# A load's last row on the other DMA queue, and one copy in place of two, in an RMSNorm that writes every row twice

## The chip, the cores and the metric

The kernel runs on one core of one Trainium2 chip. A core has engines with a queue of instructions each: TensorE (PE, not used here), VectorE (DVE), ScalarE (ACT), GpSimd (POOL) and SyncE (SP), and 16 DMA engines that move data between the memory (HBM) and the on-chip memory of 128 partitions. A DMA is issued by an instruction on SP or ACT; DMAs from SP stand in the profile as queue q1, those from ACT as queue q10. The metric is the device time in microseconds of one execution, the median of several.

## The reference

The input `x` has 8 x 512 rows of 2048 float32 values. Each row is normalised by its root mean square and multiplied by `gamma`, and every row appears twice, one after the other, in the output:

```python
x_rep = np.repeat(x, 2, axis=1)
rms = np.sqrt((x_rep ** 2).mean(axis=-1, keepdims=True) + 1e-6)
x_norm = x_rep / rms
return (x_norm * gamma[None, None, :]).astype(np.float32)
```

So 33.6 MB are read and 67.1 MB are written.

## The kernel before

The 4096 rows are cut into four loads of 1024 rows. A load puts eight consecutive rows (k = 0 to 7) into each of the 128 partitions, 8 x 8,192 bytes a partition; per DMA engine these are eight partitions. A store writes four rows with their copies, again eight rows' worth per partition and 8.4 MB, so there are eight stores. All live in one on-chip tile `y` of 24 rows per partition, with three regions that begin at rows 0 (`first`), 8 (`second`) and 16 (`third`).

The function `four` (line 93) handles two loads: load n goes to `first + K` (rows 4 to 11 of `y`), load n + 1 to `third`. It is called twice, for loads 0 and 1 (line 147) and 2 and 3 (line 148). The order of instructions on each engine is the order in which they are written; there is no scheduler. For each group of rows the steps are:

- `squares` (line 59): ACT squares each row and sums it (line 65), then takes the root of the mean of all rows of the group (line 69).
- `scale` (line 72): DVE takes the reciprocal (line 78) and, row by row, multiplies the row by it and by `gamma` (line 79), writing to every second row of the output region.
- `repeat` (line 84): ACT or DVE copies the scaled rows to the rows between (line 86).
- `store` (line 54): SP issues the store.

In the first call of `four` the first load is cut in two DMAs: rows 0 to 6 of each partition, and row 7 (`cuts` is (7, 8)). `load` (line 49) issues the pieces in reverse, so row 7 goes first, both on SP's queue; load 1 follows in one piece. ACT's queue has only gamma. The function `constants` (line 126) fetches gamma in three DMAs on it, into partition 0 of `y`: 16 pieces of 126 values, and the last 32 values in two DMAs of 64 bytes each. POOL then spreads gamma over all partitions, the main part at line 138 and the last 32 values at line 142, into `gamma_b`. Line 79 needs all of `gamma_b`.

Row 7 is first needed by the squares of the second half of load 0 (line 105, rows 7, 6, 5, 4), after the first half (rows 0 to 3, lines 99 to 104) has been scaled and copied. `at_once` is 1 in the first call and 2 in the second: there the copies of line 101 are of one row or of two.

The loads 2 and 3 are issued when the stores that read their regions have finished; the stores are issued in order on SP, as their copies are done.

Of the kernel before, what the change touches and what calls it, by code (L numbers as in the profile page):

```python
# [1 line left out]

# [4 lines left out]


@with_exitstack
def kernel(  # L10
    ctx: ExitStack,
    tc: tile.TileContext,
    x: bass.AP,
    gamma: bass.AP,
    out: bass.AP,
):
    nc = tc.nc
    P = nc.NUM_PARTITIONS
    f32 = mybir.dt.float32
    Act = mybir.ActivationFunctionType  # L20
    Alu = mybir.AluOpType

    B, S, D = x.shape
    Bo, So, Do = out.shape
    R = So // S
    assert R == 2 and D == Do and B == Bo and So == S * R
    eps = 1e-6
    inv_d = 1.0 / float(D)


    K = 4
    N = B * S
    ntiles = N // (P * K)
    assert N % (P * K) == 0 and ntiles == 8
    H = 2
    x_t = x.rearrange("b s d -> (b s) d").rearrange("(n p k) d -> n p k d", p=P, k=H * K)
    out_t = out.rearrange("b s d -> (b s) d").rearrange("(n p h j) d -> n h p (j d)", p=P, h=H, j=K * R)

    singles = ctx.enter_context(tc.tile_pool(name="singles", bufs=1))
    rows = ctx.enter_context(tc.tile_pool(name="rows", bufs=1))  # L40
    junk = ctx.enter_context(tc.tile_pool(name="junk", bufs=1, space=bass.MemoryType.PSUM))
    small = ctx.enter_context(tc.tile_pool(name="small", bufs=4))

    y = rows.tile([P, 3 * K * R, D], f32, name="y")
    first, second, third = 0, K * R, 2 * K * R

    def load(n, at, cuts=(H * K,)):
        ends = (0, *cuts)  # L50
        for k0, k1 in reversed(list(zip(ends, ends[1:]))):
            nc.sync.dma_start(out=y[:, at + k0 : at + k1, :], in_=x_t[n][:, k0:k1, :])  # L52

    def store(n, h, to):
        nc.sync.dma_start(
            out=out_t[n, h], in_=y[:, to : to + K * R, :].rearrange("p j d -> p (j d)")
        )

    def squares(at, rows):

        n = len(rows)
        ss = small.tile([P, n], f32, name=f"ss{n}")
        for c, k in enumerate(rows):
            sq = junk.tile([P, D], f32, name="sq")
            nc.scalar.activation(  # L65
                out=sq[:], in_=y[:, at + k, :], func=Act.Square, accum_out=ss[:, c : c + 1]
            )
        rms = small.tile([P, n], f32, name=f"rms{n}")
        nc.scalar.activation(out=rms[:], in_=ss[:], func=Act.Sqrt, scale=inv_d, bias=eps_t[:])  # L69
        return rms  # L70

    def scale(at, to, rows, rms, at_once=K):
        n = len(rows)
        rstd = small.tile([P, n], f32, name=f"rstd{n}")
        for c, k in enumerate(rows):
            if c % at_once == 0:
                part = slice(c, min(c + at_once, n))
                nc.vector.reciprocal(out=rstd[:, part], in_=rms[:, part])  # L78
            nc.vector.scalar_tensor_tensor(  # L79
                out=y[:, to + R * k, :], in0=y[:, at + k, :], scalar=rstd[:, c : c + 1],  # L80
                in1=gamma_b[:], op0=Alu.mult, op1=Alu.mult,
            )

    def repeat(to, k0, k1, copy):
        y_r = y[:, to + R * k0 : to + R * k1, :].rearrange("p (k r) d -> p k r d", r=R)
        copy(out=y_r[:, :, 1, :], in_=y_r[:, :, 0, :])  # L86

    ctx.enter_context(tc.manual_schedule())

    half = K // 2  # L90
    up, down = list(range(K)), list(range(K - 1, -1, -1))

    def four(n, constants, cuts, at_once):


        load(n, first + K, cuts)
        constants()
        load(n + 1, third)
        for rows, n_at_once in ((up[:half], half), (up[half:], at_once)):
            scale(first + K, first, rows, squares(first + K, rows), n_at_once)  # L100
        for k in range(0, half, at_once):
            repeat(first, k, k + at_once, nc.scalar.copy)
        repeat(first, half, K, nc.vector.tensor_copy)
        store(n, 0, first)
        scale(second, second, down, squares(second, down))
        for k in range(half, K, at_once):
            repeat(second, k, k + at_once, nc.scalar.copy)
        repeat(second, 0, half, nc.vector.tensor_copy)
        store(n, 1, second)
        roots = [squares(third + h * K, up) for h in range(H)]  # L110
        scale(third, first, up, roots[0])
        repeat(first, 0, half, nc.scalar.copy)
        repeat(first, half, K, nc.scalar.copy)
        store(n + 1, 0, first)
        scale(third + K, third, up, roots[1])
        repeat(third, 0, K, nc.scalar.copy)
        store(n + 1, 1, third)

    gamma_b = singles.tile([P, D], f32, name="gamma_b")
    G, E = 16, 2  # L120
    C = D // G - E
    gamma_s = y[0:1, 0:2, :].rearrange("p k (c d) -> p (k c) d", c=G // 2)
    gamma_t = y[0:1, 2, :]
    eps_t = singles.tile([P, 1], f32, name="eps_t")

    def constants():
        nc.gpsimd.memset(eps_t, eps)  # L127
        nc.scalar.dma_start(
            out=gamma_s[0:1, :, :C],
            in_=gamma[: G * C].rearrange("(p c d) -> p c d", p=1, c=G),  # L130
        )
        for c in range(E):
            at = G * C + c * G
            nc.scalar.dma_start(
                out=gamma_t[0:1, c * G : (c + 1) * G],
                in_=gamma[at : at + G].partition_broadcast(1),
            )
        nc.gpsimd.partition_broadcast(  # L138
            out_ap=gamma_b[:, : G * C].rearrange("p (c d) -> p c d", c=G),
            in_ap=gamma_s[0:1, :, :C],  # L140
        )
        nc.gpsimd.partition_broadcast(out_ap=gamma_b[:, G * C :], in_ap=gamma_t[0:1, : E * G])  # L142

        root = singles.tile([P, 1], f32, name="root")[:]
        nc.scalar.activation(out=root, in_=eps_t[:], func=Act.Sqrt)  # L145

    four(0, constants, (H * K - 1, H * K), 1)
    four(2, lambda: None, (H * K,), half)


# [1 line left out]
_INS = ['x', 'gamma']  # L152
_OUTS = [((8, 1024, 2048), 'float32')]


# [23 lines left out]
```

## Time and profile before

| what | value |
|---|---|
| median of 3 runs | 238.25 us (238.18 to 238.48) |
| profiled execution | 239.85 us, span 238.0 us |
| DMA, mean | 423 GB/s |
| DVE busy | 84.4 us, 35% of the span |
| ACT busy | 110.2 us, 46% |
| POOL busy | 2.9 us, 1% |
| load 0, rows 0 to 6: issue to landing | 21.5 us |
| load 0, row 7: issue to landing | 4.9 us |
| gamma, main part: issue to landing | 5.1 us |
| loads 1 to 3: issue to landing, median | 40.5 us |
| stores: issue to landing, median | 24.9 us |

The span is the time from the first to the last event of the profiled execution; 1.85 us of its time lie around the span. A busy time is the sum over an engine's instructions. The time to landing of a DMA holds its wait behind other DMAs. In the timeline each row has the start in us, the time in us, the engine (SPq and ACTq are DMA issues), the line of the kernel, the operation, its operands, how many instructions were merged in the row, and in brackets the idle time before it and what ended that. In the DMA view a queue's row has packets, MB and the time of its packets as a share of 16 engines over the window; a long packet counts where it starts.

### The profile page before, as it was taken

The numbers are of one execution on the slowest core, as the hardware profiler recorded it, in microseconds if no ns is written. First come the engines' busy times: TensorE is split into PE (matmuls) and PEld (weight loads), VectorE is DVE, ScalarE is ACT, GpSimd is POOL, SyncE is SP. The second block draws the span as 40 slices with busy tenths as digits, with TensorE's granted clock in tenths as the row PEclk, the third lists the DMA queues.
The fourth block names the chain that finished last, engine by engine and source line by source line (L and its number), as shares of the span: only waits on it lengthen the run. The fifth ranks groups of instructions, "written<-read, shape, count | busy, mean of one in ns | idle before, by whom it ended". The sixth has DMA issues, their size and how long they took to land.

```text
span 238.0 us, 228 instructions
## 1 busy us (share of the span) xinstructions
DVE 84.4 (35%) x47; ACT 110.2 (46%) x88; POOL 2.9 (1%) x7
## 2 busy tenths in 40 slices
DVE  0000495792799400000000006937918992000000
ACT  2001999299996560000000039891999957400000
POOL 0300000000000000000000000000000000000000
DMA  8997989898998989898999999999998999999994
GB/s 332 463 453 340 529 352 529 352 518 363 463 419 365 518 352 529 352 529 352 419 386 430 441 441 441 430 452 408 463 419 386 474 408 463 419 441 441 441 441 176
DMA packets 1909, 100.68 MB, mean 423 GB/s; under 512 B 244, under 2 KB 244, under 8 KB 244
## 3 DMA queue, kind: packets, MB, share of 16 engines
q1 hardware_dynamic: 1872, 100.66, 98.4%
q10 hardware_dynamic: 36, 0.01, 0.0%
q14 instruction: 1, 0.01, 0.0%
HBM read 33.56 MB, written 67.11 MB: 423 GB/s over the span
## 4 chain that ended last, share of the span: by engine, by line
DMA 46%; ACT 28%; DVE 11%; issue 1%; SPq 0%; DVEq 0%; ACTq 0%
DMA y<-in_x_dram 26%; DMA out_dram<-y 20%; ACT sq L65 17%; DVE y L79 11%; ACT y L86 11%; ACT rms L69 1%; DVE rstd L78 0%; SPq L52 0%; DVEq L79 0%; ACTq L86 0%
## 5 line engine op out<-in xcount | busy, mean ns | idle before, releaser
L65 ACT ACTIVATE sq<-y 128x2048 f32<-128x2048 f32 x32 | 60.1, 1878 | 73.2 <-DMA y<-in_x_dram 72.5
L79 DVE SCALAR_TENSOR_TENSOR y<-y,rstd,gamma_b 128x2048 f32<-128x2048 f32 x32 | 73.8, 2349 | 2.2 <-DMA out_dram<-y 1.6
L86 ACT COPY y<-y 128x4096 f32<-128x4096 f32 (+2 forms) x12 | 42.8, 3599 | 18.9 <-DVE y L79 18.9
L78 DVE RECIPROCAL rstd<-rms 128x4 f32<-128x4 f32 (+2 forms) x11 | 1.9, 169 | 111.2 <-ACT rms L69 111.2
L86 DVE COPY y<-y 128x4096 f32<-128x4096 f32 x4 | 9.2, 2293 | 0.1
L65 ACT ACTIVATION_READ_ACCUMULATOR sq<-y 128x1 f32 x32 | 6.0, 186 | 0.0
L69 ACT ACTIVATE rms<-ss,eps_t 128x4 f32<-128x4 f32 (+1 forms) x10 | 3.0, 297 | 0.3
L145 ACT ACT_TABLE_LOAD x1 | 1.3, 1283 | 2.3 <-issue 2.3
L138 POOL PARTITION_BROADCAST gamma_b<-y x1 | 2.3, 2257 | 5.1 <-DMA y<-in_gamma_dram 5.1
L142 POOL PARTITION_BROADCAST gamma_b<-y x1 | 0.3, 310 | 6.2 <-DMA y<-in_gamma_dram 6.2
L145 ACT ACTIVATE root<-eps_t 128x1 f32<-128x1 f32 x1 | 0.2, 203 | 0.0
L127 POOL MEMSET eps_t<- 128x1 f32 x1 | 0.1, 98 | 0.3 <-POOLq L163 0.3
L163 POOL MEMSET const-bfloat16-1.0<- 128x1 bf16 x1 | 0.1, 101 | 0.0
L163 POOL MEMSET const-uint8-127<- 128x1 uint8 x1 | 0.1, 101 | 0.0
L163 POOL MEMSET const-float32-0.0<- 128x1 f32 x1 | 0.1, 98 | 0.2 <-issue 0.2
L163 POOL MEMSET const-float32-1.0<- 128x1 f32 x1 | 0.1, 98 | 0.0
## 6 DMA issues: line engine op xcount, KB each, us to landing
y<-in_x_dram SPq DMA_DIRECT2D x1, 7168.0 KB, 21.5
y<-in_x_dram SPq DMA_DIRECT2D x1, 1024.0 KB, 4.9
out_dram<-y SPq DMA_DIRECT2D x8, 24.9
y<-in_x_dram SPq DMA_DIRECT2D x3, 40.5
y<-in_gamma_dram ACTq DMA_DIRECT2D x2, 0.1 KB
y<-in_gamma_dram ACTq DMA_DIRECT2D x1, 7.9 KB, 5.1
```

The costliest lines, as they stand in the source:

```text
L65: nc.scalar.activation(out=sq[:], in_=y[:, at + k, :], func=Act.Square, accum_out=ss[:, c : c + 1])
L69: nc.scalar.activation(out=rms[:], in_=ss[:], func=Act.Sqrt, scale=inv_d, bias=eps_t[:])
L78: nc.vector.reciprocal(out=rstd[:, part], in_=rms[:, part])
L79: nc.vector.scalar_tensor_tensor(out=y[:, to + R * k, :], in0=y[:, at + k, :], scalar=rstd[:, c : c + 1], in1=gamma_b[:], op0=Alu.mult, op ...
L86: copy(out=y_r[:, :, 1, :], in_=y_r[:, :, 0, :])
L127: nc.gpsimd.memset(eps_t, eps)
L138: nc.gpsimd.partition_broadcast(out_ap=gamma_b[:, : G * C].rearrange("p (c d) -> p c d", c=G), in_ap=gamma_s[0:1, :, :C],)
L142: nc.gpsimd.partition_broadcast(out_ap=gamma_b[:, G * C :], in_ap=gamma_t[0:1, : E * G])
L145: nc.scalar.activation(out=root, in_=eps_t[:], func=Act.Sqrt)
L163: nc = _bacc.Bacc("TRN2", target_bir_lowering=False, num_devices=1)
```

## The change

The first load still has two pieces, but they are issued in rising order and on two queues: rows 0 to 6 on SP's, row 7 on ACT's. As `load` is called ahead of `constants`, row 7 stands before gamma's three DMAs there. Loads with one piece go on SP's queue as before. The second edit replaces the loop over the first two copies on ACT by a single copy of two rows; it differs only in the first call of `four`, since the second call already copied two rows at once.

```diff
     def load(n, at, cuts=(H * K,)):
         ends = (0, *cuts)
-        for k0, k1 in reversed(list(zip(ends, ends[1:]))):
-            nc.sync.dma_start(out=y[:, at + k0 : at + k1, :], in_=x_t[n][:, k0:k1, :])
+        for k0, k1, queue in zip(ends, cuts, (nc.sync, nc.scalar)):
+            queue.dma_start(out=y[:, at + k0 : at + k1, :], in_=x_t[n][:, k0:k1, :])
...
-        for k in range(0, half, at_once):
-            repeat(first, k, k + at_once, nc.scalar.copy)
+        repeat(first, 0, half, nc.scalar.copy)
         repeat(first, half, K, nc.vector.tensor_copy)
```

## The prediction

> **What bounds the kernel now.** I read the page first: the span, the slices of the DMA engines, the queues.
>
> ```profile
> span 238.0 us, 228 instructions
> DMA  8997989898998989898999999999998999999994
> q1 hardware_dynamic: 1872, 100.66, 98.4%
> q10 hardware_dynamic: 36, 0.01, 0.0%
> ```
>
> The 16 DMA engines are busy in every slice. SyncE's queue, q1, holds 98.4% of their time; DVE and ACT are at 35% and 46%. The kernel is a stream of 100.66 MB that is never let run dry, so an edit costs time only where it lets the stream stop. The chain of waits (46% DMA, 28% ACT) runs back through compute because each store is issued by compute, but no gap shows there. So the second reading is where the stream is nearest to stopping. That is the first store, whose data must pass through compute while load 1 is still landing. The timeline of that stretch:
>
> ```profile
> 0.72 1.34 SPq L52 DMA_DIRECT2D y<-in_x_dram  x3
> 0.72 0.60 ACTq L128 DMA_DIRECT2D y<-in_gamma_dram  x1
> 1.35 0.91 ACTq L134 DMA_DIRECT2D y<-in_gamma_dram  x2
> 5.92 2.26 POOL L138 PARTITION_BROADCAST gamma_b<-y  x1 [5.12 <-DMA y<-in_gamma_dram]
> 14.36 0.31 POOL L142 PARTITION_BROADCAST gamma_b<-y  x1 [6.18 <-DMA y<-in_gamma_dram]
> 22.69 1.88 ACT L65 ACTIVATE sq<-y 128x2048 f32<-128x2048 f32 x1 [18.90 <-DMA y<-in_x_dram]
> 27.35 4.62 DVE L79 SCALAR_TENSOR_TENSOR y<-y,rstd,gamma_b 128x2048 f32<-128x2048 f32 x2
> 31.22 3.68 ACT L86 COPY y<-y 128x2048 f32<-128x2048 f32 x2
> 36.92 2.29 DVE L86 COPY y<-y 128x4096 f32<-128x4096 f32 x1
> 39.29 16.20 SPq L55 DMA_DIRECT2D out_dram<-y  x2
> ```
>
> gamma is spread over the partitions by 14.67 us and is first used at 27.35: 12.7 us of room. The first store is issued at 39.29. A cold queue needed 1.01 us from issue (0.72) to its first packet (1.73, packet records), so the store could start at 40.30. The packet records show load 1 leaving the 16 engines between 40.96 and 41.48. The room before the stream stops is therefore 0.66 to 1.18 us; I take 0.85.
>
> The third reading decides: how the two queues share an engine. DMA view for three windows, 1.5 to 4.6, 4.6 to 5.2 and 5.2 to 14.0 us (columns: packets, MB, share):
>
> ```profile
> q1 hardware_dynamic: 122, 1.00, 92.8%
> ...
> q1 hardware_dynamic: 38, 0.97, 375.7%
> q10 hardware_dynamic: 32, 0.01, 6.0%
> ...
> q1 hardware_dynamic: 64, 3.67, 96.2%
> q10 hardware_dynamic: 4, 0.00, 0.0%
> ```
>
> The packet records give the order inside these windows. On each engine it is: row 7's eight packets of 8,192 bytes (0.306 us each) and its 4-byte semaphore write; gamma's 504 bytes and its semaphore write; then the packets of rows 0 to 6, 57,344 bytes and 2.113 us each. So no gamma packet came between row 7's, although both DMAs were issued at 0.72. On the one engine that carries gamma's two last pieces their four packets (64 B, 4 B, 64 B, 4 B) go one at a time behind one 57,344-byte packet each. That is why line 142 starts only at 14.36. Two rules follow: a DMA whose issue is done first (SP's took 0.37 us, ACT's 0.60) gets its nine packets in first; once both queues are backed up they alternate packet by packet, whatever the sizes.
>
> **The change part by part.** First part: SP loses one of its first three issues (row 7, 0.37 us) and starts with rows 0 to 6 at 0.72. ACT gains row 7's issue, and gamma's three move behind it, in time and in q10. Bytes and packets stay the same. On one engine load 0 and load 1 need 8 x 2.113 + 8 x 0.306 + 8 x 2.414 = 38.7 us however they are mixed, so load 1 still leaves at about 41.2. The landing of rows 0 to 6 moves from 22.67 to between 19.5 (row 7 wholly behind) and 22.6 (mixed). An earlier landing buys nothing if gamma is what comes last. One issue less on SP buys nothing either: the queue is full at once.
>
> What is late next is gamma. q10 now holds, on the engine with the last pieces, 15 packets: row 7's nine, gamma's two, then four. q1 holds nine of rows 0 to 6 and nine of load 1 (eight of 65,536 bytes, 2.414 us, and the semaphore write), and then nothing until the first store, which itself needs gamma. By the first rule, SP's nine packets of rows 0 to 6 pass first, as SP's nine of row 7 did before: both DMAs start at 0.72 again. Then row 7's alternate with load 1's. If no more than six of q10's 15 slip through ahead of that, nine or more remain against load 1's nine, so gamma's last piece gets in when load 1 is through, at about 41.2. From its packet to line 142 took 0.72 us (13.64 to 14.36), line 142 takes 0.31, the hop 0.05: DVE starts at 42.3 in place of 27.35. That is 14.95 us later; the 0.85 of room comes off: 14.1 us in which the DMA engines have nothing.
>
> Bounds of this unknown: gamma could stay early (row 7 wholly ahead, as in the trace of before; cost 0), or even gamma's main piece could be done only when load 1 is through on all engines. Then line 138 starts at 41.48 + 0.72 = 42.2, and 2.26 + 0.31 + 0.05 more make DVE start at 44.8, a cost of 17.45 - 0.85 = 16.6. I take 14.1, which lies between the mixtures below and that end. Nothing lies below zero: DMA work is the same and the stream has no gap that an earlier row could close.
>
> Who waits while gamma is late: DVE's first multiply, behind it all of DVE's queue; on ACT the copy of line 86, and behind it the squares of the second half; POOL has nothing else; SP stands at the first store.
>
> Second part: on ACT two copies (3.68 us together) become one of 4096 elements, 3.60 by the by-form groups (mean 3598 ns): 0.1 us less. But it waits for both multiplies: its start moves from 3.87 us after DVE's start (31.22 - 27.35, ACT was busy until then) to 4.67, and its end from 7.55 to 8.27, so the squares of the second half start 0.7 to 0.8 us later. The first store waits for DVE's copy (11.9 after DVE's start), so it is not touched. The second store is issued 27.8 us after DVE's start now, 28.6 then, and its packets could start at 29.6; the first store keeps the engines until 12.9 + 8 x 2.414 = 32.2. Hidden, with 2.6 us to spare; if that cover were gone it would cost 0.8. The third store (75.52 now, 1.0 to its packets, the second's last packets end at 79.9) has 3.4 us now and keeps 1.7.
>
> The sum goes on the profiled execution's own time: 239.85 (span 238.0 and 1.85 around it) + 14.1 + 0 = 253.95. The median of the runs is 1.60 under the profiled one: 252.35, say 252.4.
>
> **A rule weighed.** The rows say one packet at a time (64 bytes against 57,344). The Trainium skill, "DMA: Bandwidth & Descriptors", section "Queues, rings and completion order", says that each DMA engine goes round its queues and drains a whole packet, typically 9 to 17 descriptors, before it switches. By that rule row 7 would go as one turn, and all of load 1 as one turn ahead of gamma, which is the second rival below, 254.9. In this trace the order of row 7 and gamma fits that rule; the four pieces between single 57,344-byte rows do not.
>
> **The rivals.**
> One by one from the first packet on. For it: the last pieces were let in after a single 57,344-byte packet. Against: row 7's nine went ahead of gamma undivided. If one packet of rows 0 to 6 leads, the 15th packet of q10 follows the 15th of q1, which is the sixth of load 1: 1.73 + 0.5 (the first packets took up to 1.1 us, not 0.31) + 16.9 + 2.4 + 6 x 2.414 = 36.0, DVE at 37.1, cost 9.75 - 0.85 = 8.9: 247.2. With a lead of two: 249.6. With three or more: 252.4. With ACT ahead by one packet: 244.8.
>
> Whole transfers in turn. All of load 1 passes before gamma's main piece, or too few of row 7's nine slip through: 238.25 + 16.6 = 254.9.
>
> No change: row 7 gets its nine packets in before rows 0 to 6 do. For it: both issues start at 0.72, and small packets are soon done (2.5 us). Then gamma has six packets against eight of rows 0 to 6 and is there by 1.73 + 0.5 + 2.4 + 8 x 2.113 = 21.5 at the latest, DVE-ready at 22.6, under 27.35. The time is then 238.2. It decides at a gamma_b ready before 27.35 + 0.85 = 28.2. Against: SP's issue took 0.37 us and ACT's 0.60, side by side. Letting one queue drain several small packets per turn would do the same; the four single pieces speak against it.
>
> **How the numbers follow.** Gamma behind load 1: 0.57, of which 0.32 for 252.4 (the likeliest) and 0.25 for 254.9, 0.10 of that for whole transfers in turn. One by one: 0.27 (0.13 near 249.6, 0.10 near 247.2, 0.04 near 244.8). No change: 0.16. The range leaves out no change and the 0.04: 246.8 to 255.3, which holds 0.8. A change under 0.2% (0.5 us) is about what a measurement of this kernel cannot tell from none. No change is split over both sides of zero: faster 0.04, since nothing in the stream shortens, same 0.12; slower 0.84. The slower cases' own range is 244.5 to 255.3.
>
> **What would show it.** Line 142 of before (141 after) starts near 41.9 and not 14.36; the first multiply waits for POOL and starts near 42.3; the first store is issued near 54.2; the DMA slices show one gap, from about 41 to 55, and are full after it. Landing of rows 0 to 6 tells who led: near 19.5 SP, near 22.5 mixed. Wrong would be a gamma_b ready before 28, and the prediction's first rule with it.

## The result and the profile after

The changed kernel takes 248.21 us (median of 5, 248.11 to 248.39) against 238.25 us: a ratio of 1.0419, 95% interval 1.0405 to 1.0433. It is 9.96 us slower. Forecast was 252.4 with 246.8 to 255.3; the direction and the place are as forecast, and the time is that of a rival, 247.2 plus 1.0 us. It lies in the range only because the range took in that rival, to which the prediction gave a chance of 0.10.

The same stretch of the timeline, of the kernel after (start, us, engine, line, operation, count, idle time before it and what ended that; rows between these are left out):

```profile
0.71 0.42 ACTq L52 DMA_DIRECT2D y<-in_x_dram  x1
0.72 0.85 SPq L52 DMA_DIRECT2D y<-in_x_dram  x2
22.88 1.88 ACT L65 ACTIVATE sq<-y 128x2048 f32<-128x2048 f32 x1 [18.64 <-DMA y<-in_x_dram]
27.81 2.26 POOL L137 PARTITION_BROADCAST gamma_b<-y  x1 [27.00 <-DMA y<-in_gamma_dram]
37.30 0.31 POOL L141 PARTITION_BROADCAST gamma_b<-y  x1 [7.24 <-DMA y<-in_gamma_dram]
37.65 4.62 DVE L79 SCALAR_TENSOR_TENSOR y<-y,rstd,gamma_b 128x2048 f32<-128x2048 f32 x2 [10.20 <-POOL gamma_b L141]
42.34 3.60 ACT L86 COPY y<-y 128x4096 f32<-128x4096 f32 x1 [10.84 <-DVE rstd L78]
49.58 16.95 SPq L55 DMA_DIRECT2D out_dram<-y  x2
```

Rows 0 to 6 land as before (first squares at 22.88, 22.69 before). What is new stands in the brackets: the second broadcast waits for gamma until 37.30, the first multiply waits 10.20 us for the broadcast, and ACT's copy 10.84 us for the multiplies. The first store is issued 10.29 us later than in the profile of before. The page shows what that does to the stream:

```profile
span 246.4 us, 227 instructions
DMA  8999894098979797979997979999898979899994
q1 hardware_dynamic: 1728, 99.62, 94.0%
q10 hardware_dynamic: 180, 1.06, 1.0%
```

One slice is empty and its neighbour half empty. The windows view narrows it down (stretch, its length, busy us and instructions of each engine, clock, DMA share, GB/s):

```profile
38.00:41.00 3.00, 3.00 (x2) 0.00 (x0) 0.00 (x0) 1.00 0.81 350
41.00:44.00 3.00, 2.96 (x3) 1.66 (x1) 0.00 (x0) 1.00 0.00 0
44.00:47.00 3.00, 2.96 (x3) 3.00 (x2) 0.00 (x0) 1.00 0.00 0
47.00:50.00 3.00, 2.48 (x2) 2.94 (x5) 0.00 (x0) 1.00 0.00 0
50.00:53.00 3.00, 0.00 (x0) 2.97 (x3) 0.00 (x0) 1.00 1.53 655
```

Load 1 is through at 41.0 to 41.9 and the first store's packets start at 50.42. In between no packet of data starts. Everything after it is the old stream, moved, but for half a microsecond where the stores give way to load 2, which is taken up below.

How the queues were mixed shows in the DMA view of three windows, 1.5 to 4.4, 4.4 to 6.8 and 24.0 to 26.5 us (packets, MB, share):

```profile
q1 hardware_dynamic: 16, 0.92, 97.3%
...
q1 hardware_dynamic: 16, 0.92, 88.2%
q10 hardware_dynamic: 16, 0.13, 12.9%
...
q1 hardware_dynamic: 16, 1.05, 97.2%
q10 hardware_dynamic: 16, 0.01, 1.1%
```

One packet of rows 0 to 6 goes ahead on each of the 16 engines. From then on each round has one packet of SP's queue and one of ACT's per engine, whether that one has 8,192 bytes or, in the last window, 504. Gamma's main piece goes just ahead of the second packet of load 1; the four packets of its end start, by the records, at 29.31, 31.73, 34.15 and 36.58, one round of 2.42 us apart.

One remark on the numbers: in the profiled execution of before half of the engines fell behind by up to 1.5 us where the stores give way to load 2 (116 to 123 us). A second profile of that kernel, below, has a time of 238.02 and a span of 236.2 without that, and is the better partner for the changed kernel, whose engines stay together there: 246.4 - 236.2 = 10.2 us between profiles, 9.96 between medians.

### The profile page after: what moved, and what is told of

Its sections match the earlier page's. It is cut to its first block, busy times and chain, and to the rows that moved or that the text cites. A ratio compares the mean times of both kernels' runs of the same rounds, so it can differ in the third digit from the quotient of the medians.

```text
span 246.4 us, 227 instructions
## 1 busy us (share of the span) xinstructions
DVE 84.5 (34%) x47; ACT 110.3 (45%) x87; POOL 2.9 (1%) x7
## 4 chain that ended last, share of the span: by engine, by line
DMA 48%; ACT 23%; DVE 12%; issue 2%; ACTq 1%; POOLq 0%; DVEq 0%
DMA out_dram<-y 18%; DMA y<-in_x_dram 16%; DMA y<-in_gamma_dram 14%; ACT sq L65 13%; DVE y L79 12%; ACT y L86 10%; ACT rms L69 0%; ACTq L133 0%; DVE rstd L78 0%; ACTq L127 0%; ACTq L52 0%; POOLq L173 0%; DVEq L79 0%; POOLq L141 0%
## 5 line engine op out<-in xcount | busy, mean ns | idle before, releaser
L79 DVE SCALAR_TENSOR_TENSOR y<-y,rstd,gamma_b 128x2048 f32<-128x2048 f32 x32 | 73.8, 2349 | 11.4 <-POOL gamma_b L141 10.2
```

The lines of the kernel that those rows point to most:

```text
L79: nc.vector.scalar_tensor_tensor(out=y[:, to + R * k, :], in0=y[:, at + k, :], scalar=rstd[:, c : c + 1], in1=gamma_b[:], op0=Alu.mult, op ...
```

## The experiments

**The queues alone.** The two short copies stay.

```diff
-        repeat(first, 0, half, nc.scalar.copy)
+        for k in range(0, half, at_once):
+            repeat(first, k, k + at_once, nc.scalar.copy)
```

> The change's first part alone: rows 0 to 6 on SP's queue, row 7 on ACT's ahead of gamma; the two copies of one row stay. Theory (gamma alternates packet by packet behind row 7 and comes too late): 248.2 us as with both parts, first multiply at 37.6, first store issued at 49.6; the copies cost nothing (within 0.3). Rival (the longer copy, which holds back the squares of the second half by 0.8 us, is part of the loss): 247.4 to 247.9.

248.12 us (247.92 to 248.26), span 246.4; the first multiply and the first two stores:

```profile
37.57 4.61 DVE L79 SCALAR_TENSOR_TENSOR y<-y,rstd,gamma_b 128x2048 f32<-128x2048 f32 x2 [10.19 <-POOL gamma_b L142]
...
49.51 15.20 SPq L55 DMA_DIRECT2D out_dram<-y  x2
```

The queues are the whole loss. In the runs beside this one the kernel before has a median of 239.63 and not 238.25, so that the loss is 8.49 us there (ratio 1.0367, interval 1.0333 to 1.0401) and not 9.96: it is the time of before that varies. The second store is issued 14.85 us after the first here and 16.61 after it in the full change, so the longer copy does hold it back by 1.8 us, and that is hidden, as the first store's packets are still going.

**The copy alone.** The kernel before with the one long copy.

```diff
-        for k in range(0, half, at_once):
-            repeat(first, k, k + at_once, nc.scalar.copy)
+        repeat(first, 0, half, nc.scalar.copy)
```

> The change's second part alone: one copy of two rows in place of two, the DMAs as before. Theory (hidden by more than 2 us under the first store): 238.2 us, the second store issued up to 0.8 us later than the 55.1 of before. Rival (it is not hidden): 239.0.

Medians of 239.58 us and, for the kernel before on the same chip, 239.63; the ratio on record is 1.0009, interval 0.9988 to 1.0031. The runs of before spread from 238.0 to 240.2 there, so 0.2% either way can't be told. The second store comes 16.6 us after the first, 15.9 in the second profile of before: 0.7 later, hidden.

**Before once more.**

> The kernel before once more, for a second profile of it. Theory: the first profiled execution of before lost about 1.5 us at the first change from stores to loads (116 to 123 us), where half of the DMA engines fell behind, and this one's span is near 236.4. Rival: the delay belongs to the kernel and the span is 238.0 again.

238.02 us, span 236.2. By the packet records the step from the last store packets to load 2's took 2.65 us in the mean and no engine fell behind. So the delay in the first profile is not in every execution of before. It is not in that one alone either: in the profile of the copy alone (239.49 us, span 237.7) one engine starts load 2 at 120.13, 1.1 us after the last of the others, and stays behind to the end. Of the runs of before beside it 22 of 25 took 239.1 to 240.2 us, which fits such a delay in most of them; as they have no trace, that is not shown, nor is what sets it off.

**Gamma ahead of row 7.** The change, with ACT's DMAs in the other order.

```diff
-        load(n, first + K, cuts)
         constants()
+        load(n, first + K, cuts)
```

> As changed, but gamma's three DMAs stand ahead of row 7 on ACT's queue. Theory (the loss is gamma's place behind row 7's nine packets): gamma's six packets go behind the first six of rows 0 to 6, the line of the second broadcast starts near 16, the first multiply near 27.4, 238.2 us; row 7 lands late, near 37, and holds up only the squares of the second half by about 1 us, which is hidden. Rival (two queues that share the engines cost time whatever the order, or the mixed landing of rows 0 to 6 does): 240 to 248.

240.08 us, 1.0031 of before with 1.0012 to 1.0051. Beside the 248.12 of the queues alone, on the same chip, 8.04 of the 8.49 us are gone, with two queues that still share the engines, so it is gamma's place that cost them. gamma is spread by 18.5 and the first multiply starts at 26.55:

```profile
18.20 0.31 POOL L141 PARTITION_BROADCAST gamma_b<-y  x1 [6.11 <-DMA y<-in_gamma_dram]
...
26.55 4.62 DVE L79 SCALAR_TENSOR_TENSOR y<-y,rstd,gamma_b 128x2048 f32<-128x2048 f32 x2
```

The rest was not as expected. Row 7 now stands behind gamma. On most engines its packets take turns with the last of rows 0 to 6 and the first of load 1; on the engine with gamma's end all eight come after rows 0 to 6, six of them between packets of load 1, the last at 36.28:

```profile
39.59 1.88 ACT L65 ACTIVATE sq<-y 128x2048 f32<-128x2048 f32 x1 [4.75 <-DMA y<-in_x_dram]
...
80.30 0.33 SPq L55 DMA_DIRECT2D out_dram<-y  x1
```

The squares of the second half wait 4.75 us for it, not 1, and the third store is issued at 80.30, too late: between the second and the third store the packet starts are 3.11 us apart in the mean and not 2.42, a gap of 0.7 us. The hidden room at the third store was 3.4 us by the prediction, and 5 us of lateness went through it.

**One end piece, three end pieces.** The change with E = 1 or E = 3 in place of 2: gamma's end in one or three DMAs of 64 bytes, two packets fewer or more on one engine.

```diff
-    G, E = 16, 2
+    G, E = 16, 1
```

> As changed, but gamma's end is fetched in one DMA and not in two (E = 1: 127 of 128 values in each main piece, one piece of 64 bytes). Two packets fewer on ACT's queue. Theory (one packet of that queue per 65,536-byte packet of load 1, 2.414 us each): the last broadcast starts 4.83 us earlier, near 32.5, and the time is 248.2 - 4.8 = 243.4. Rival (gamma's delay goes by bytes, or by row 7 landing whole): 248.2.

> As changed, but gamma's end is fetched in three DMAs of 64 bytes (E = 3). Two packets more on ACT's queue. Theory (one packet per 65,536-byte packet): the last broadcast starts 4.83 us later, near 42.1, and the time is 248.2 + 4.8 = 253.0. Rival: 248.2.

The second broadcast of the one, then of the other:

```profile
32.48 0.29 POOL L141 PARTITION_BROADCAST gamma_b<-y  x1 [2.57 <-DMA y<-in_gamma_dram]
```

```profile
42.22 0.32 POOL L141 PARTITION_BROADCAST gamma_b<-y  x1 [12.38 <-DMA y<-in_gamma_dram]
```

32.48, 37.30, 42.22: steps of 4.82 and 4.92 us for two packets of 64 and 4 bytes. The times are 243.59, 248.21 and 253.18: steps of 4.6 and 5.0. 68 bytes cost two packets of 65,536 bytes on the other queue. Gamma's delay goes by packets, not by bytes, and past the room at the first store it is the time of the kernel.

**Rising order on one queue.** Rows 0 to 6, then row 7, both on SP; gamma alone on ACT. It asks how many packets get ahead of the other queue's first.

```diff
-        for k0, k1, queue in zip(ends, cuts, (nc.sync, nc.scalar)):
+        for k0, k1, queue in zip(ends, cuts, (nc.sync, nc.sync)):
```

> Both pieces of the first load on SP's queue, rows 0 to 6 first and then row 7; gamma alone on ACT's. It asks who goes ahead in the first microseconds. Theory one (the DMA whose issue ends first gets its nine packets in whole, as row 7's nine did before): gamma's packets come behind all eight of rows 0 to 6, the main broadcast starts at 20 or later. Theory two (with packets of 57,344 bytes only one gets ahead): gamma's main piece lands behind the first two, the main broadcast starts near 8 and the last one near 16. Time 238.2 by both, since gamma is needed at 27.4.

Theory one is refuted, and theory two is off by one packet. The DMA view from 1.5 to 6.5 and from 6.5 to 8.6 us has

```profile
q1 hardware_dynamic: 32, 1.84, 97.0%
...
q1 hardware_dynamic: 16, 0.92, 101.0%
q10 hardware_dynamic: 16, 0.01, 1.2%
```

two packets of 57,344 bytes per engine, then one of gamma's, then one each in turn; the broadcasts start at 9.89 and 18.08, where theory two had 8 and 16. The time is 239.25, 0.9989 of before (0.9973 to 1.0005). Rows 0 to 6 land 2 us earlier and the first store is issued at 36.99, 2.3 us earlier than in the first profile of before. Nothing comes of it.

**Rows of two.** The same with the cut after row 2.

```diff
-    four(0, constants, (H * K - 1, H * K), 1)
+    four(0, constants, (2, H * K), 1)
```

> Both pieces of the first load on SP's queue, rows 0 and 1 first (16,384-byte packets) and then rows 2 to 7 (49,152 bytes); gamma alone on ACT's queue. How many packets of SP's first DMA get ahead of gamma's first? Eight of 8,192 bytes did in the kernel before, two of 57,344 did with rows 0 to 6 first. Theory (it goes by bytes or time, 64 to 115 KB an engine): 4 to 7 of 16,384. Rival (by DMA or by packets: all eight, or two).

A single run, 239.27 us. From 1.5 to 5.3 us and from 5.3 to 5.9 the view has

```profile
q1 hardware_dynamic: 80, 1.31, 97.9%
...
q1 hardware_dynamic: 16, 0.26, 104.5%
q10 hardware_dynamic: 16, 0.01, 5.3%
```

five packets of 16,384 bytes per engine ahead of gamma, 82 KB. Two of 57,344 are 115 KB, and all eight of 8,192 are 66 KB. The head start is a span of bytes or of time and no count of packets; which of the two, these runs do not tell.

**A later first store.** The rising order left a question: why is an earlier store worth nothing? In its records the last packet of load 1 on each engine took 3.5 to 3.8 us, not 2.42. So it was run again beside a kernel with more work ahead of the first store, VectorE's copy done twice.

```diff
         repeat(first, half, K, nc.vector.tensor_copy)
+        if n == 0:
+            repeat(first, half, K, nc.vector.tensor_copy)
         store(n, 0, first)
```

> Both pieces of the first load on SP's queue in rising order, once more, as the partner of the next kernel on the same chip. Its first store was issued at 37.0 us and the last packets of load 1 then took 3.5 to 3.8 us each in place of 2.42: the same again.

> The same with VectorE's copy ahead of the first store done twice, which adds 2.3 us of work and moves the first store's issue from 37.0 to about 39.3. Theory (a store that is queued before the last packets of load 1 slows these packets; issued just as they begin, it does not): the last packets of load 1 take about 2.45 us, the first store's packets start about 1.2 us earlier than in the partner, near 41.2 in the mean and not 42.6, and the time is 0.8 to 1.2 us less although there is more work. Rival (the slow packets come from the order on the queue or from chance): no difference in the time, the packets slow again.

The store's issue and the landing of load 1, first without and then with the second copy (DMA issues: count, us from issue to landing):

```profile
36.85 0.35 SPq L55 DMA_DIRECT2D out_dram<-y  x1
...
y<-in_x_dram SPq DMA_DIRECT2D x1, 41.5
```

```profile
39.15 0.35 SPq L55 DMA_DIRECT2D out_dram<-y  x1
...
y<-in_x_dram SPq DMA_DIRECT2D x1, 40.5
```

With the second copy the store comes 2.3 us later, load 1 lands 1.0 us earlier, its last packets take 2.44 us in the mean and not 3.63, and the first store's packets start at 41.29 in the mean, not 42.47. The span is 236.2 with it and 237.3 without; the times are 238.52 (238.15 to 240.47) with it and 239.16 (238.93 to 239.57) without, over 12 runs each. The 0.64 between the medians is less than the 0.8 to 1.2 expected. Part of that shows in the records: the kernel without the second copy passes from the stores to load 2 with no delay (a step of 2.42 us, 2.66 with it) and wins 0.24 back there. Against before the kernel with the second copy is at 0.9979, interval 0.9954 to 1.0004: no kernel here is shown to beat before.

## Why the prediction was right or wrong

*The bound and the place: right.* The stream stops once, at the first store, and is full after it. The lateness passes through line 141, DVE, ACT and SP as named.

*The second part at nothing: right.* In the kernel before the copy moves the second store by 0.7 us, forecast 0.7 to 0.8, and no time; alone it is 1.0009. With gamma late it is 1.8 us, since the two short copies no longer waited for ACT; still hidden.

*The first rule: wrong, and with it the 252.4.* The step was "SP's nine packets of rows 0 to 6 pass first, as SP's nine of row 7 did before". One passed. The two cases looked alike (SP's first DMA, nine packets, both issued at 0.72) and differed in two things that the step left out. Row 7's packets are a seventh in size: 66 KB against 459 KB an engine, and the two runs with rising order have 115 and 82 KB as the most that got ahead of gamma. And ACT's issue took 0.60 us for gamma's pattern but 0.42 for row 7's: it ended 0.04 us after SP's first (0.37 us) and not 0.2, so there was hardly a lead to use. The sum of 14.1 us rested on this step, and the cost was that of one packet ahead in place of nine. That the shorter lead made it one packet and not two fits, but no run separates it.

*The second rule: right.* Packet by packet, whatever the sizes. The rival made of it with a lead of one had gamma's last packet follow the sixth packet of load 1; it does, at 36.58. The two sizes of gamma's end show the price of a packet directly.

*The rival's 247.2 was 1.0 us short.* Two terms. Gamma: the first packets took up to 3.06 us each. On the engine with gamma's end load 1 began at 21.85, 0.3 us later than the rival's terms have it (21.53, with 0.5 for slow first packets), and its six packets ahead of gamma's last took 14.73 us and not 14.48; DVE started at 37.65, not 37.1. And the room of 0.85: against the second profile of before the multiply is 10.60 us late and the first store's packets start 9.17 us late, so the room there was larger, 1.4; 0.3 of it is that the last packets of load 1 took 2.72 us there and 2.42 after the change. But 0.5 us were lost again where the stores give way to load 2 (two steps of 3.07 and 2.52 us against 2.65 and 2.42), and the engines end 0.3 us further apart. Why that turn costs 0.5 us more after the change is open; the queues alone show it too (3.12), and so does gamma ahead of row 7 (3.13). It is not the change's alone: the first profile of before has 3.09, and with both pieces on SP in rising order it is 2.42.

*Whole transfers in turn: refuted.* In the changed kernel, behind the first packets of rows 0 to 6, rows of 8,192 bytes and more, the pieces of 504 and 64 bytes and even the 4-byte semaphore writes go one at a time. The 254.9 did not come. The Trainium skill, "DMA: Bandwidth & Descriptors", section "Queues, rings and completion order", has each engine drain a whole packet of typically 9 to 17 descriptors before it turns to the next queue. If each packet of the profile is one such descriptor, which no run here can tell, the changed kernel does not agree with it. Only the start of the kernel before, where row 7's nine and then gamma's first two go undivided, has an order that fits; five of 16,384 or two of 57,344 bytes went ahead in the other runs.

*No change: refuted* by one packet of lead: SP's issue did end first, though by 0.04 us only.

*"Nothing lies below zero, an earlier landing buys nothing": right for a reason that the prediction did not have.* A first store that is issued earlier slows the last packets of the load before it, by 1.2 us where it was issued at 36.9.

## What to carry to other kernels

Where a small transfer shares the DMA engines with large ones, count the packets that stand ahead of it on its own queue: each costs one packet of the other queue, here 2.4 us for 4 bytes. Put what is needed first at the head of its queue, fetch it in few DMAs, and keep bulk rows off that queue or behind it, but then ask who needs these rows, as row 7 showed. In a stream that is already full, find the one place where compute and stream nearly meet; here the slack there was about a microsecond, and all but that of the 10 us of lateness was paid.

## What was not expected of the hardware

A store that is already queued slows the last reads ahead of it. With the first store issued at 36.9 to 37.0 us the last 65,536-byte packet of load 1 on each engine took 3.6 to 3.7 us in the mean in place of 2.42; issued at 38.5, 2.9; at 39.0, 2.7; at 39.15 with the extra copy, 2.44; at 39.29 in the first profile of before, and in the changed kernel with no store queued, 2.42. Earlier than 36.9 adds little: issued at 34.5, in the kernel with rows of two, 3.7, and the packets before the last kept their 2.42. The pair of kernels that differ only in the extra copy, one profile each, shows that it is the time of issue. What the two directions contend for, no run here shows.
